# The first unit of the up projections with B22 third, x parts split from PSUM copies, weight sums ahead of the norm, and a later load of x in the down projections

## The chip, the core and the metric

The program runs on one core of one Trainium2 chip. The metric is the device time of one execution in microseconds (us), median of the runs shown. Six engines' rows appear below: PE (TensorE, matmuls), DVE (VectorE), ACT (ScalarE), POOL (GpSimd), SP (SyncE, which issues the DMAs); PEld is PE's weight load.

## What is computed

Two decoder layers over 1024 tokens with 1024 channels, all in float32. The feed-forward part of each layer, where the change lies, is, cut to what matters:

```python
def swiglu(h, w_gu, w_down):
    gu = h @ w_gu
    g, u = jnp.split(gu, 2, axis=-1)
    return (jax.nn.silu(g) * u) @ w_down

x = x + mixer(rms_norm(x, ...))          # layer 0: gMLP, layer 1: attention
x = x + swiglu(rms_norm(x, ffn_norm[l]), ffn_w_gu[l], ffn_w_down[l])
```

The width of g and of u is 2816 (22 blocks of 128 columns, 11 pairs).

## The kernel before

Every float32 operand is split in two: ACT makes `hi` (a rounded copy, `split` L162, L163), DVE makes `lo` = source - hi (L164), and PE does three matmuls for each product of blocks: hi hi, hi lo, lo hi. On top of that the projections use Strassen's scheme in Winograd's form: seven products instead of eight for a 2 x 2 split of the operands. On the side of x the seven operands are B11 and B21 (quarters of x), B22 (the fourth quarter), T1 = B11 - B12 and the sums T2, T3, T4 that are built on it; on the side of the weights a11, a12, a22 and S1 to S4, sums of quarters made on POOL (`sums` L324, `sum4` L336).

`ffn_up` (L242) goes over 11 pairs j of column blocks, for gate (gu = 0) and up (gu = 1). The first, j = 0, is the *first unit* (`unit` L353): it is computed product by product while the operands of x are still being made, since it follows the mixer's out projection and the norm. Later pairs (`pair` L450) find the operands ready. A product is 12 matmuls, 4 parts k by 3; a part needs hi and lo of that part (tiles such as T2h, T2l, by `put` L258) and the weights of the product (tile wg, hi and lo, by `weight` L300). The weights arrive in tiles `graw` (1 MB for each j and gu, two of them, `raw0` and `raw1`).

The norm is a scale of columns of x. `Entry` (L817) adds each finished tile of the out projection to x (`post`, L826), spills it (L827), squares it on ACT, and sums the squares on POOL, the last one on DVE (`Norm.add` L137). PE sums over partitions (`col`), DVE adds epsilon (nm, L146), POOL takes the power (nr, L150), PE spreads it as a row in PSUM, and `entry.scale` (L160, DVE) multiplies a tile of x by that row. There are two halves of tokens; B11 and B21 come from the first half, whose norm is ready early, the rest needs the second half's. The differences for T1 to T4 are taken in place on x by POOL (`difference` L263, L264; one, T2's last, on DVE).

What sets the order: a scheduler orders each engine's instructions by priority and dependence, and lists given to `T.order` fix DVE's and POOL's order around the first unit (L278 to L292, L549 to L565). Each engine runs its instructions in that order, so one that waits holds those behind it.

`ffn_down` (L604) multiplies the activations (in DRAM, `ascr`, written tile by tile by `store` L343 and `store_sums` L351) with the down weights, again in seven products. The first activation operand `a0` has two tiles, 5 blocks in `a0` and 6 in `a0b`; SP issues its loads, those of the weights and those of x (`new_x` L107, eight tiles of 512 KB from the spill `xscr`, L112) in one queue. The cuts hi and lo are L645 (ACT) and L646 (DVE), the sums of results into x are L681. Where x is loaded is one line:

```python
            with tc.issue_after(load(W4, weight(1, 1)).ins):
                xt = new_x(xscr)
            X = four(psp[0])
            product(X, A0, W2, True, 0, (W2, W3, W2))
            load(A0, act(2))
            add(X, 0, 0)
```

## Time and profile before

| | |
|---|---|
| median of 3 runs | 2198.87 us (2197.94 to 2204.6) |
| the profiled execution | 2199.69 us, its span 2198.0 |
| mean granted clock of PE | 0.988 |
| PE busy | 2111.9 us, 96% |
| DVE, ACT, POOL busy | 1444.8 (66%), 1213.7 (55%), 979.6 us (45%) |
| chain that ended last | PE 78%, DVE 12%, DMA 3% |
| matmuls | 10640 |
| DMA | 265.85 MB, mean 121 GB/s |

Times are from the start of the span. A row of a timeline has the start, the busy time, the engine and line, the operation, the tiles (out<-in) and, in brackets, the idle time of the engine before it with what released it. Busy times are shares over stages with different limits, so what a change is worth is read in its own stage. The granted clock is 1.00 at 2.4 GHz and 0.50 at 1.2 GHz.

### The profile page before, as it was taken

How to read it: one execution, taken by the hardware profiler on the slowest of the kernel's cores; microseconds unless marked ns; L12 is line 12 of the kernel's file. 1: busy time of each engine (PE TensorE's matmuls, PEld its weight loads, DVE VectorE, ACT ScalarE, POOL GpSimd, SP SyncE). 2: the span in 40 equal slices, each digit the busy share in tenths (PEclk: the TensorE clock that was granted, in tenths of full speed). 3: DMA queues.
4: the chain of work that ended last, by engine and by line, in shares of the span. 5: the costliest groups of instructions: out<-in, count | busy, mean ns of one | idle time of the engine just before them, and what ended most of it. 6: DMA issues, size and time to landing. Idle time of an engine off the chain costs nothing.

```text
span 2198.0 us, 30179 instructions
## 1 busy us (share of the span) xinstructions
PE 2111.9 (96%) x10640; PEld 1769.8 (81%) x10640; DVE 1444.8 (66%) x2541; ACT 1213.7 (55%) x2436; POOL 979.6 (45%) x856
## 2 busy tenths in 40 slices
PE   9999888999999979999999999999799999999998
PEld 7888666888888768878888888887588888887887
DVE  5545988545555656775288898865955555458685
ACT  5323355766676534453177777743466767664463
POOL 5023668675767400234122332204885757660024
PEclk9999999999999989999999999999999999999999
DMA  4230022232323853235423324573123223259413
GB/s 164 64 114 35 23 92 72 97 110 101 112 97 114 292 205 132 103 110 163 114 72 92 92 77 117 195 250 138 54 91 110 98 101 115 92 193 347 136 48 105
DMA packets 111320, 265.85 MB, mean 121 GB/s; under 512 B 10400, under 2 KB 20640, under 8 KB 104256
## 3 DMA queue, kind: packets, MB, share of 16 engines
q1 hardware_dynamic: 93808, 224.98, 29.5%
q0 software_dynamic: 17360, 38.93, 6.3%
q8 instruction: 84, 1.38, 0.3%
q14 instruction: 68, 0.56, 0.1%
HBM read 179.47 MB, written 77.07 MB: 117 GB/s over the span
## 4 chain that ended last, share of the span: by engine, by line
PE 78%; DVE 12%; DMA 3%; issue 2%; ACT 2%; POOL 2%; SPq 0%; DVEq 0%; POOLq 0%; ACTq 0%
PE mm L39 54%; PE d L39 15%; PE sc L39 3%; PE po L39 3%; PE tr L42 2%; DVE cut L646 1%; DVE wg L164 1%; DVE w_hi L164 1%; DVE w_lo L164 1%; DVE E L1241 1%; PE tr L39 1%; DMA x<-xscr 1%; DMA a0b<-ascr 1%; DVE fine L164 1%; DVE E L1253 1%
## 5 line engine op out<-in xcount | busy, mean ns | idle before, releaser
L39 PE MATMUL d<-cut 128*128 128x512 f32 (+1 forms) x1788 | 407.2, 388 | 24.2 <-ACT cut L645 15.0
L39 PEld LDWEIGHTS d<-cut 128*128 128x128 f32 x1788 | 331.8, 189 | 96.4 <-ACT cut L645 15.4
L137 POOL TENSOR_TENSOR acc<-acc,sq 128x512 f32<-128x512 f32 (+1 forms) x64 | 92.6, 1448 | 381.2 <-ACT sq L133 379.5
L462 DVE TENSOR_TENSOR c<-c,mm 128x256 f32<-128x256 f32 (+1 forms) x300 | 150.4, 507 | 159.0 <-PE mm L39 128.6
L309 DVE TENSOR_TENSOR wg<-row,wg 128x512 fp32r<-128x512 f32 x180 | 116.7, 658 | 91.8 <-ACT wg L308 87.9
L39 PE MATMUL mm<-hT_hi,w_hi 128*128 128x512 f32 x384 | 155.9, 406 | 0.0
L39 PE MATMUL mm<-hT_hi,w_lo 128*128 128x512 f32 x384 | 151.4, 394 | 0.0
L39 PE MATMUL mm<-hT_lo,w_hi 128*128 128x512 f32 x384 | 150.9, 393 | 0.0
L645 ACT CAST cut<-a 128x512 fp32r<-128x512 f32 x110 | 68.1, 621 | 138.5 <-PE d L39 136.2
L39 PE MATMUL mm<-fine,wg 128*128 128x256 f32 x960 | 138.0, 283 | 2.5 <-DVE c L462 1.2
L39 PEld LDWEIGHTS mm<-fine,wg 128*128 128x128 f32 x960 | 129.8, 190 | 12.9 <-ACT wg L308 2.6
L321 ACT COPY c<-mm 128x512 f32<-128x512 f32 x152 | 88.9, 585 | 80.3 <-PE mm L39 48.5
L646 DVE TENSOR_TENSOR cut<-a,cut 128x512 fp32r<-128x512 f32 x110 | 88.8, 807 | 61.1 <-ACT cut L645 60.8
L331 POOL TENSOR_TENSOR S<-graw 128x512 f32<-128x512 f32 x44 | 59.3, 1349 | 153.8 <-DMA graw<-in_w_gu 153.8
L39 PE MATMUL mm<-B11h,wg 128*128 128x512 f32 x352 | 118.7, 398 | 4.5 <-DVE wg L164 3.4
L39 PE MATMUL mm<-T1h,wg 128*128 128x512 f32 x352 | 117.4, 395 | 5.4 <-DVE wg L309 4.4
L308 ACT CAST wg<-S 128x512 fp32r<-128x512 f32 x160 | 98.4, 620 | 39.1 <-PE mm L39 31.0
L39 PE MATMUL mm<-B22h,wg 128*128 128x512 f32 x352 | 117.6, 396 | 2.2 <-DVE wg L164 1.8
L39 PE MATMUL mm<-T2h,wg 128*128 128x512 f32 x352 | 117.6, 396 | 0.5 <-DVE wg L164 0.5
L1245 ACT ACTIVATE E<-E,nm 128x256 f32<-128x256 f32 (+7 forms) x128 | 99.6, 778 | 33.3 <-DVE nm L1241 31.5
L308 ACT CAST wg<-graw 128x512 fp32r<-128x512 f32 x160 | 99.4, 623 | 32.0 <-PE mm L39 29.4
L350 POOL TENSOR_TENSOR c<-c,c 128x512 f32<-128x512 f32 x88 | 115.8, 1326 | 0.9 <-PE mm L39 0.7
(287 smaller groups left out, 5787.8 us busy)
## 6 DMA issues: line engine op xcount, KB each, us to landing
graw<-in_w_gu SPq DMA_DIRECT2D x44, 1024.0 KB, 4.9
ascr<-c SPq DMA_DIRECT2D x154, 256.0 KB, 2.0
a<-ascr SPq DMA_DIRECT2D x12, 1280.0 KB, 6.6
a<-ascr SPq DMA_DIRECT2D x18, 768.0 KB, 4.9
xscr<-x SPq DMA_DIRECT2D x48, 256.0 KB, 2.1
w<-in_w_down SPq DMA_DIRECT2D x14, 768.0 KB, 7.9
a0b<-ascr SPq DMA_DIRECT2D x12, 768.0 KB, 7.5
x<-xscr SPq DMA_DIRECT2D x16, 512.0 KB, 11.8
```

Source lines behind the costliest of these rows:

```text
L39: return self._keep(self.engine.matmul(*args, **kw))
L137: return (V if last else G).tensor_tensor(self.acc, self.acc, part, op=ALU.add)
L164: return V.tensor_tensor(lo, src, hi.bitcast(F32), op=ALU.subtract)
L308: A.copy(w[:, 0], src)
L309: T.note(line, name, V.tensor_tensor(w[:, 1], near, w[:, 0].bitcast(F32), op=ALU.subtract))
L321: A.copy(r, src)
L331: T.note(line, ("S1", layer, j, gu), G.tensor_tensor(s1, a21, a22, op=ALU.add))
L350: G.tensor_tensor(to, x, y, op=op_)
L462: V.tensor_tensor(c, c, ps, op=ALU.add)
L645: A.copy(o[:, 0], src)
L646: T.note(line, name + ("lo",), V.tensor_tensor(o[:, 1], src, o[:, 0].bitcast(F32), op=ALU.subtract))
L1245: A.activation(Em[:, :L], Em[:, :L], AF.Exp, scale=-1.0, bias=nm, accum_out=acc)
```

## The change

1. In the first unit the products come in the order B11, B21, B22, T1, T2, T3, T4 (before: B11, B21, T1, T2, T3, B22, T4). B22's part k is scaled by the norm and split at once; T2 then finds its tile scaled. The result c12 starts with B22's product, and T1's and T2's are added to it.
2. `put` gets a place `near` in PSUM for T1 to T4: ACT copies the part of x there as well, and DVE's split reads the copy instead of x in SBUF. The weights of T3 and T4 go the same way, as those of later pairs do.
3. All weight sums of j = 0 are made ahead of the norm in POOL's order; those of gu = 1 lie in a tile `early` that lends its room from T4 (layer 0) or T3 (layer 1), and the splits of B22's weights stand ahead of the scales on DVE.
4. `raw0` and `raw1` of layer 0 lie where room comes free early, and SP issues both `graw` loads ahead of all sixteen spills of x of the mixer (before: behind twelve). The splits of the weights of B11 and B21 then stand among the out projection's operands on DVE. In layer 1 they stand behind the third add on x instead of the second. The pool of weight tiles has 6 (layer 0) and 5 (layer 1) buffers instead of 4, and the accumulators of the squares have tiles of their own.
5. In both down projections x is loaded behind `load(A0, act(2))` instead of behind the load of W4.

The diff, without the parts that only follow from this (unchanged lists, the move of two definitions, and the old lists of order):

```diff
@@ -243,20 +243,29 @@
...
-            order = (("B11", "T1", "T2", "T3", "B22", "S", "w1", "s1"), ("s", "T4", "B21", "raw0", "raw1"))
+            order = (("B11", "T1", "raw0", "raw1", "T2", "T3", "B22", "w1"), ("T4", "s", "B21", "S", "s1"))
             if layer:
                 order = (("w1", "raw1", "raw0", "B11", "T1", "T2", "T3", "B21", "S"), ("T4", "s", "B22", "w2", "s1"))
-            ps = {n: (pool, right)[side](st, f"g{n}{layer}", {"w1": 4, "w2": 2}.get(n, 1)) for side in range(2) for n in order[side]}
+            ps = {n: (pool, right)[side](st, f"g{n}{layer}", {"w1": 5 if layer else 6, "w2": 2}.get(n, 1)) for side in range(2) for n in order[side]}
...
+            early_at = "T3" if layer else "T4"
...
-                hi[n] = p.tile([P, 4, 512], F32R, name=n + "h")
+                if n != early_at:
+                    hi[n] = p.tile([P, 4, 512], F32R, name=n + "h")
...
-            def put(n, k, src):
-                T.note(line, ("lo", layer, n, k), split(hi[n][:, k], lo[n][:, k], src))
+            early = ps[early_at].tile([P, 4, 4, P], F32, name="early", tag="early")
+
+            def put(n, k, src, near=None):
+
+                if near is not None:
+                    A.copy(near, src)
+                A.copy(hi[n][:, k], src)
+                src = src if near is None else near
+                T.note(line, ("lo", layer, n, k), V.tensor_tensor(lo[n][:, k], src, hi[n][:, k].bitcast(F32), op=ALU.subtract))
 
...
-                "B11": lambda k: entry.scale(k, 0), "B21": lambda k: entry.scale(k + 4, 0), "B22": lambda k: xt[k + 4][:, h1],
+                "B11": lambda k: entry.scale(k, 0), "B21": lambda k: entry.scale(k + 4, 0), "B22": lambda k: entry.scale(k + 4, 1),
...
-                "T2": lambda k: difference(("T2", k), xt[k][:, h0], entry.scale(k + 4, 1), xt[k][:, h0]),
+                "T2": lambda k: difference(("T2", k), xt[k][:, h0], xt[k + 4][:, h1], xt[k][:, h0]),
...
+            n_raw, n_stage = [0], [0]
+            spare = pool(st, "spare", 1, space=PSUM) if layer else None
+
+            def stage():
+                n_stage[0] += 1
+                return spare.tile([P, 512], F32, name="near") if layer and n_stage[0] % 2 else entry.row(0)
+
...
-                for n in ("B11", "B21", "T1", "T2"):
+                for n in ("B11", "B21", "B22", "T1", "T2"):
                     for k in range(4):
-                        put(n, k, sources[n](k))
+                        put(n, k, sources[n](k), stage() if n[0] == "T" else None)
...
                 w = (ps["w2"] if layer and name[-1] == "B22" else w1).tile([P, 2, *src.shape[1:]], F32R, name="wg")
-                if name[1] == layer and name[2] == 0:
+                if name[1] == layer and name[2] == 0 and name[-1] not in ("T3", "T4"):
...
@@ -327,7 +336,8 @@
...
-                s4, s3, s2, s1 = (sp.tile([P, 4, P], F32, name=n) for n in ("S4", "S3", "S2", "S1"))
+                s4, s3, s2, s1 = (sp.tile([P, 4, P], F32, name=n) if j or not gu else early[:, i]
+                                  for i, n in enumerate(("S4", "S3", "S2", "S1")))
...
+                sum4(0, gu, a12, s2, s4)
+                SRC[gu] = {"T3": s3, "T4": a22}
                 Z, Y, X = (p.tile([P, 512], F32, name="mm") for p in mmp)
                 product(X, a11, "B11", True)
                 c11 = snap(f"c11{gu}", X, 2 - gu)
...
+                product(Y, s4, "B22", True)
+                c12 = snap(f"c12{gu}", Y)
+                yield
                 product(Z, s1, "T1", True)
                 c22 = snap(f"c22{gu}", Z)
-                sum4(0, gu, a12, s2, s4)
+                T.note(line, ("c12", layer, 0, gu), V.tensor_tensor(c12, c12, Z, op=ALU.add))
                 yield
                 product(X, s2, "T2", False)
-                c12 = snap(f"c12{gu}", X)
+                V.tensor_tensor(c12, c12, X, op=ALU.add)
+                multiply(X, (yield), "T3", False, (layer, 0, gu, "T3"))
+                V.tensor_tensor(c22, c22, X, op=ALU.add)
+                multiply(X, (yield), "T4", False, (layer, 0, gu, "T4"))
+                res += [c11, c12, X, c22]
...
-                product(X, s3, "T3", False)
-                V.tensor_tensor(c22, c22, X, op=ALU.add)
-                yield
-                product(Z, s4, "B22", False)
-                V.tensor_tensor(c12, c12, Z, op=ALU.add)
-                yield
-                product(X, a22, "T4", False)
-                res += [c11, c12, X, c22]
...
+            SUMS, SRC = {}, {}
...
@@ -533,7 +544,7 @@
...
-            for b in ("B11", "B21", "T1", "T2"):
+            for b in ("B11", "B21", "B22", "T1", "T2"):
...
-            for n in ("T3", "B22", "T4"):
+            for n in ("T3", "T4"):
+                ws = [weight(SRC[gu][n], ("w", layer, 0, gu, n)) for gu in range(2)]
+                if n == early_at:
+                    hi[n] = ps[n].tile([P, 4, 512], F32R, name=n + "h", tag="early")
                 for k in range(4):
-                    put(n, k, sources[n](k))
+                    put(n, k, sources[n](k), stage())
                 for gu in range(2):
-                    next(first[gu], None)
...
+                    first[gu].send(ws[gu])
+            sc, lo_, w = (lambda k: ("scale", layer, 1, k)), (lambda n, k: ("lo", layer, n, k)), (lambda n, gu: ("w", layer, 0, gu, n))
...
+            names = [w("B22", 0), w("B22", 1), sc(4), sc(5), lo_("B22", 0), sc(6), sc(7), lo_("B22", 1), sc(0), c11_(0), lo_("B22", 2), sc(1),
+                     lo_("B22", 3), c11_(1), sc(2), sc(3), w("T1", 0), lo_("T1", 0), lo_("T1", 1), w("T1", 1), lo_("T1", 2), lo_("T1", 3), w("T2", 0)]
+            names += [lo_("T2", k) for k in range(3)] + [("d", layer, "T2", 3), lo_("T2", 3), w("T2", 1), c12_(0), c12_(1)]
+            for n in ("T3", "T4"):
+                names += [w(n, 0), w(n, 1)] + [lo_(n, k) for k in range(4)]
             T.order(line, names)
...
+            names = [("S4", layer, 0, 0)] + [(f"S{i}", layer, 0, 1) for i in (1, 2, 3, 4)]
+            names += [("d", layer, "T1", k) for k in range(4)] + [("d", layer, "T2", k) for k in range(3)]
+            names += [("d", layer, n, k) for n in ("T3", "T4") for k in range(4)]
...
             X = four(psp[0])
             product(X, A0, W2, True, 0, (W2, W3, W2))
-            load(A0, act(2))
+            with tc.issue_after(load(A0, act(2)).ins):
+                xt = new_x(xscr)
...
-        acc = hp[1].tile([P, 2, 512], F32, name="acc", tag="hT")
-        norms = [Norm(HALF[h], acc[:, h], sq) for h in range(2)]
+        norms = [Norm(HALF[h], tp.tile([P, 512], F32, name=f"acc{h}", tag=("vh", "vl")[h]), sq) for h in range(2)]
...
```

Three places in the order of instructions, before and after.

SP at the start of layer 0's down projection, before (w_6715 is W4, a_6711 the first tile of a0, a0b its second, a_6713 the tile of a1, c the stored results of the last pair of columns):

```order
L112 DMA x<-xscr_83 128x1024
L343 DMA ascr_87<-c_6311 128x512
L112 DMA x<-xscr_83 128x1024 x4
L343 DMA ascr_87<-c_6475 128x512
L112 DMA x<-xscr_83 128x1024
L351 DMA ascr_87<-c_6424 128x512
L112 DMA x<-xscr_83 128x1024 x2
L351 DMA ascr_87<-c_6369 128x512
L600 DMA a_6711<-ascr_87 128x5x512
L351 DMA ascr_87<-c_6495 128x512
L351 DMA ascr_87<-c_6497 128x512
L600 DMA a0b<-ascr_87 128x3x512 x2
```

and after:

```order
L361 DMA ascr_87<-c_6464 128x512
L353 DMA ascr_87<-c_6351 128x512
L361 DMA ascr_87<-c_6535 128x512
L361 DMA ascr_87<-c_6409 128x512
L611 DMA a_6751<-ascr_87 128x5x512
L353 DMA ascr_87<-c_6515 128x512
L361 DMA ascr_87<-c_6537 128x512
L611 DMA a0b<-ascr_87 128x3x512 x2
L611 DMA a_6753<-ascr_87 128x5x512
L611 DMA a_6753<-ascr_87 128x3x512 x2
L611 DMA a0b<-ascr_87 128x3x512
L112 DMA x<-xscr_83 128x1024 x8
```

The eight loads of x stood between the stores and ahead of the loads of a0b; they now stand behind all three loads of a0b, the last of which belongs to the third product.

DVE behind the norm of the second half in layer 0, before (row is the norm's row in PSUM, x_132 to x_135 the tiles of the fourth quarter, x_136 to x_139 those of the second):

```order
L146 TENSOR_SCALAR nm4_2336<-row_2331 128x4
L160 SCALAR_TENSOR_TENSOR x_136<-x_136,fgain0_333,row_2330 128x512
L160 SCALAR_TENSOR_TENSOR x_137<-x_137,fgain0_333,row_2330 128x512
L160 SCALAR_TENSOR_TENSOR x_138<-x_138,fgain0_333,row_2330 128x512
L160 SCALAR_TENSOR_TENSOR x_139<-x_139,fgain0_333,row_2330 128x512
L164 TENSOR_TENSOR wg_2563<-S1_2478,wg_2563 128x512
L164 TENSOR_TENSOR T1l_2408<-x_136,T1h_2407 128x512
L160 SCALAR_TENSOR_TENSOR x_132<-x_132,fgain0_333,row_2330 128x512
L164 TENSOR_TENSOR T1l_2408<-x_137,T1h_2407 128x512
L160 SCALAR_TENSOR_TENSOR x_133<-x_133,fgain0_333,row_2330 128x512
L164 TENSOR_TENSOR T1l_2408<-x_138,T1h_2407 128x512
```

and after:

```order
L146 TENSOR_SCALAR nm4_2337<-row_2332 128x4
L160 SCALAR_TENSOR_TENSOR x_132<-x_132,fgain0_333,row_2331 128x512
L160 SCALAR_TENSOR_TENSOR x_133<-x_133,fgain0_333,row_2331 128x512
L268 TENSOR_TENSOR B22l_2413<-x_132,B22h_2412 128x512
L160 SCALAR_TENSOR_TENSOR x_134<-x_134,fgain0_333,row_2331 128x512
L160 SCALAR_TENSOR_TENSOR x_135<-x_135,fgain0_333,row_2331 128x512
L268 TENSOR_TENSOR B22l_2413<-x_133,B22h_2412 128x512
L160 SCALAR_TENSOR_TENSOR x_136<-x_136,fgain0_333,row_2331 128x512
L375 TENSOR_TENSOR c110_2526<-c110_2526,mm_2509 128x512
L268 TENSOR_TENSOR B22l_2413<-x_134,B22h_2412 128x512
L160 SCALAR_TENSOR_TENSOR x_137<-x_137,fgain0_333,row_2331 128x512
L268 TENSOR_TENSOR B22l_2413<-x_135,B22h_2412 128x512
```

The splits of T1 from x were the first to follow; now B22's four parts do, with two scales ahead of each of the first two, and a sum of results among them.

POOL ahead of the same norm, before (acc the norm's accumulator, S the weight sums of gu = 0, nr4 the power):

```order
L137 TENSOR_TENSOR acc_1681<-acc_1681,sq_2317 128x512
L137 TENSOR_TENSOR acc_1681<-acc_1681,sq_2322 128x512
L331 TENSOR_TENSOR S1_2478<-graw_2473 128x512
L333 TENSOR_TENSOR S3_2476<-graw_2473 128x512
L150 TENSOR_TENSOR nr4_2338<-nm4_2336,mhalf_75 128x4
L332 TENSOR_TENSOR S2_2477<-S1_2478,graw_2473 128x512
L337 TENSOR_TENSOR S4_2475<-graw_2473,S2_2477 128x512
```

and after (early holds the sums of gu = 1):

```order
L341 TENSOR_TENSOR S1_2503<-graw_2498 128x512
L343 TENSOR_TENSOR S3_2501<-graw_2498 128x512
L342 TENSOR_TENSOR S2_2502<-S1_2503,graw_2498 128x512
L347 TENSOR_TENSOR S4_2500<-graw_2498,S2_2502 128x512
L341 TENSOR_TENSOR early_2417<-graw_2528 128x512
L137 TENSOR_TENSOR acc1_1682<-acc1_1682,sq_2313 128x512
L342 TENSOR_TENSOR early_2417<-early_2417,graw_2528 128x512
L343 TENSOR_TENSOR early_2417<-graw_2528 128x512
L137 TENSOR_TENSOR acc1_1682<-acc1_1682,sq_2318 128x512
L347 TENSOR_TENSOR early_2417<-graw_2528,early_2417 128x512
L137 TENSOR_TENSOR acc1_1682<-acc1_1682,sq_2323 128x512
L150 TENSOR_TENSOR nr4_2339<-nm4_2337,mhalf_75 128x4
```

Two sums stood between the last accumulation and the power; now eight stand among the last three accumulations.

## Rows read from the trace of the kernel before

**Rows 1.** PE's waits, whole run (engine, line, tile; releaser: us in all, times, longest)

```profile
PE d L39 <- ACT cut L645: 15.0, 1, 15.0
...
PE mm L39 <- DVE x L826: 3.8, 1, 3.8
```

**Rows 2.** Slices of the first unit, layer 0 (busy us, granted clock, DMA share, GB/s)

```profile
300.00:310.00 10.00, 5.98 (x17) 4.12 (x16) 10.00 (x14) 4.80 (x9) 6.05 (x5) 0.68 0.57 208
...
330.00:340.00 10.00, 6.65 (x16) 4.17 (x17) 10.00 (x10) 5.67 (x11) 8.17 (x6) 0.72 0.00 0
```

**Rows 3.** Timeline of PE, then of ACT, start of layer 0's down projection

```profile
754.90 13.01 PE L39 MATMUL d<-cut 128*128 128x512 f32 x56 [2.28 <-DVE cut L646]
782.88 7.38 PE L39 MATMUL d<-cut 128*128 128x512 f32 x20 [14.97 <-ACT cut L645]
...
782.21 1.66 ACT L645 CAST cut<-a0b 128x512 fp32r<-128x512 f32 x3 [13.65 <-DMA a0b<-ascr]
```

**Rows 4.** Timeline of SP's DMA issues, first unit and down projection, layer 0

```profile
295.85 0.81 SPq L328 DMA_DIRECT2D graw<-in_w_gu  x2
...
762.81 1.58 SPq L112 DMA_DIRECT2D x<-xscr  x2
...
769.81 1.53 SPq L600 DMA_DIRECT2D a0b<-ascr  x2
...
784.79 0.36 SPq L600 DMA_DIRECT2D a0b<-ascr  x1
```

**Rows 5.** Page, part 6: DMA issues (KB each, median us to landing)

```profile
a0b<-ascr SPq DMA_DIRECT2D x12, 768.0 KB, 7.5
x<-xscr SPq DMA_DIRECT2D x16, 512.0 KB, 11.8
```

**Rows 6.** Slice of the down projection's start, layer 0

```profile
750.00:790.00 40.00, 22.75 (x88) 17.92 (x87) 20.35 (x28) 9.40 (x17) 4.22 (x3) 0.79 1.04 397
```

**Rows 7.** Timeline of PE, first unit of layer 0

```profile
305.49 1.22 PE L39 MATMUL mm<-B11h,wg 128*128 128x512 f32 x2 [3.44 <-DVE wg L164]
...
319.94 0.40 PE L39 MATMUL mm<-T1h,wg 128*128 128x512 f32 x1
...
363.58 0.40 PE L39 MATMUL mm<-B11h,wg 128*128 128x512 f32 x1
```

**Rows 8.** Timeline of DVE, end of out projection and first unit, layer 0

```profile
295.11 0.68 DVE L164 TENSOR_TENSOR w_lo<-wo,w_lo 128x512 fp32r<-128x512 f32 x1
...
308.85 0.68 DVE L137 TENSOR_TENSOR acc<-acc,sq 128x512 f32<-128x512 f32 x1
...
314.57 2.72 DVE L160 SCALAR_TENSOR_TENSOR x<-x,fgain,row 128x512 f32<-128x512 f32 x4 [1.85 <-PE row L42]
...
331.76 1.75 DVE L164 TENSOR_TENSOR T2l<-x,T2h 128x512 fp32r<-128x512 f32 x1
```

**Rows 9.** Timeline of POOL, first unit of layer 0

```profile
313.80 1.27 POOL L332 TENSOR_TENSOR S<-S,graw 128x512 f32<-128x512 f32 x1
...
331.25 6.78 POOL L264 TENSOR_TENSOR x<-x 128x512 f32<-128x512 f32 x4
```

**Rows 10.** PE's waits, 301 to 370, layer 0

```profile
PE mm L39 <- DVE T2l L164: 3.7, 3, 2.4
PE mm L39 <- DVE T1l L164: 2.1, 3, 0.7
...
PE mm L39 <- DVE T4l L164: 1.5, 3, 1.1
```

**Rows 11.** Groups of ACT's instructions, copies into PSUM (busy us, mean ns, idle before)

```profile
L307 ACT COPY row<-S 128x512 f32<-128x512 f32 x80 | 47.2, 591 | 17.4 <-POOL S L332 9.5 <-DVE wg L309 5.5 <-POOL S L331 1.1
```

**Rows 12.** Timeline of DVE, out projection of layer 1

```profile
1494.27 6.20 DVE L164 TENSOR_TENSOR wg<-graw,wg 128x512 fp32r<-128x512 f32 x4 [7.13 <-ACT wg L163]
```

**Rows 13.** PE's waits, 1535 to 1600, layer 1

```profile
PE mm L39 <- DVE T2l L164: 3.4, 3, 1.9
...
PE mm L39 <- DVE T1l L164: 1.8, 3, 0.7
```

25 lines of the change are left out of this document (3 added, 22 removed).

## Prediction

> **What bounds the kernel now.** I read the page's shares first: PE is nearly always busy, so a change that leaves the matmuls as they are can only win back what PE waits, and what it loses at half clock. The table of PE's waits over the whole run comes next [rows 1]: one wait of 15.0 us for a cut on ACT stands alone, and one of 3.8 us for a sum of x. Both lie where this change works. The slices of the first unit of layer 0 [rows 2] show that PE there loses speed too: the granted clock is 0.68 in 300 to 310 and 0.72 in 330 to 340, while DVE is busy for 10.00 of 10 us in both. DVE sets the pace of this unit, and PE, which stutters behind it, drops to half clock.
>
> The 15-us wait is read from the start of layer 0's down projection [rows 3]: PE is through its last operands at 782.88 - 14.97 = 767.91; ACT's casts of the second part of `a0` (a0b) start at 782.21, after 13.65 us for a DMA. The issue times [rows 4] say why: the eight loads of x, the last two from 762.81, are issued ahead of the a0b loads at 769.81. They are 512 KB each [rows 5], 4.19 MB, and the DMA is full from 750 to 790, at 397 GB/s [rows 6], so all that is queued lands in its turn.
>
> **The change, part by part.** The sum is made against the profiled execution, 2199.69 us (span 2198.0 and 1.7 around it); the median shown, 2198.87, is 0.8 below.
>
> *Down projection, layer 0.* The x loads move behind a0b and the loads of the next product. The 4.19 MB at 0.397 MB/us are some 10.5 us that no longer stand ahead of a0b: it lands near 771.7 instead of 782.2, and PE's wait shrinks from 15.0 to some 4.5. **-10.5.** Upper bound of the gain: the whole wait, and the half clock behind it (20 matmuls take 7.38 us where 56 take 13.01 [rows 3], so 20 should take 4.65): -15.0 - 2.7 = -17.7. Lower bound: a0b's own issue doesn't come before 769.81, since the stores that it reads stay ahead of it, and it lands after a load's median of 7.5 us on the page [rows 5], at 777.3: -4.9. I take the value between, since the DMA was full for the whole stretch [rows 6]: bytes decide there, not issue times. x itself is needed at the first add on x, by the order behind the fifth operand of product 1. It is now issued behind the a0b load that stood at 784.79 [rows 4], some 10.5 earlier, about 774.3, and all eight land within 11.8 [rows 5], by 786. That add would come near 784 and needs the first of the eight: covered, but by a few us only; if the cover is gone, see the first rival. In layer 1 the same move meets no wait of size: 0, between -2 and +2.
>
> *Weights of the first two products, layer 0.* PE waited 3.44 for B11's weights, up to 305.49 [rows 7], and ran at half clock behind it (0.68 for that slice, so 3.2 of 10 us [rows 2], of which the wait itself has a part): some 6 in all. The loads of these weights stood at 295.85 on SP [rows 4], behind twelve spills of x; now they stand ahead of all of them, and the four splits on DVE stand among the operands of the out projection. If DVE has no gap in that stretch they cost 4 x 0.68 = 2.7 there (a split alone, the row at 295.11 [rows 8]); at 1.75, which a split takes beside POOL [rows 8], 7.0. I take 2.7, the nearer row, as it is of the same stretch.
>
> *The norm, layer 0.* Against this: POOL now makes eight weight sums among the norm's last three accumulations. The tiles of these sums come free with the split that ends at 295.8 [rows 8], or 298.5 with the 2.7 above. Eight sums and three accumulations of the same size, at 1.27 alone to 1.70 beside DVE (6.78 for four) [rows 9], are 14.0 to 18.7 us: POOL is through at 312.5 to 317.2, and the last accumulation on DVE, at 308.85 before [rows 8], comes 3.7 to 8.4 later. From there to the first scale at 314.57 [rows 8] lay 5.7 us, in part PE's other matmuls ahead of the norm's; I count 4.5 to 5. The first scale comes at 317 to 322, and the first product of B22 two later, at 319 to 324, where the third product began at 319.94 [rows 7]. PE has B11 and B21 (48 matmuls of 0.232 [rows 3], 11.1 us) until about 315, then it idles. Third product: -0.8 to +4.1, taken **+1.5**. What was won on B11's weights is thus spent before the norm.
>
> *From the third product to the next unit, layer 0.* Before: 319.94 to 363.58 [rows 7], 43.6 us for five products, 120 matmuls, of which 27.8 are due. The waits named T1l, T2l and T4l are 2.1, 3.7 and 1.5 [rows 10], 7.3 in all. A split of T2 from SBUF takes 1.75 beside POOL [rows 8]; scales, with a PSUM operand, take 0.68 each there (2.72 for four) [rows 8], although POOL starts its differences within them. So T1 to T4 with x read from PSUM come to about 0.65 each and these waits go, with half the lost clock of the slice 330 to 340 (0.28 of 10 us, so 1.4): about -9. Against it: B22, third now, keeps its splits from SBUF, and each part of it needs two scales and a split on DVE, 2 x 0.68 + 0.68 to 1.75 = 2.0 to 3.1 us, where PE takes 0.7: three waits of 1.3 to 2.4, +4 to +7. I take +4. **-5**, bounds -9 and +2. The sums for the T3 and T4 weights read PSUM as well; that's in the -9.
>
> *The copies.* Sixteen copies into PSUM per layer on ACT, and four for T3's and T4's weights, at 0.591 [rows 11]: 9.5 and 2.4 us of ACT, which is busy for 4.80 and 5.67 of 10 us [rows 2]. It hides them; without cover, the copy for the first part of each of T1 to T4 would show, 4 x 0.6 = 2.4 per layer. The two extra adds on c12 (0.6 each) end beside matmuls.
>
> *Layer 1.* DVE worked 6.20 us on four weight splits, which had waited 7.13 for ACT's casts of the loaded weights [rows 12], and the add on x for which PE waited 3.8 [rows 1] stood behind them. Now one more add stands ahead of the splits; the first part is there in time, so the 3.8 go, **-4** with a little clock (bounds -6 and 0). In the unit the waits for T2l and T1l are 3.4 and 1.8 [rows 13], -5.2, and some clock, -1.5; B22 costs +4 as above, and two more sums ahead of the norm (2 x 1.27 to 1.70) delay it by 2.5 to 3.4, of which 2.2 show: **-0.5**, bounds -7 and +6.
>
> Sum: -10.5 + 1.5 - 5 - 4 - 0.5 = -18.5: 2199.69 - 18.5 = 2181.2, less the 0.8 to the median: **2180.4 us**.
>
> **A rule weighed.** DVE's splits beside POOL take 1.75 and POOL's operations 1.70 instead of 1.27 [rows 8, 9]: both go on, one of each in turn, and a scale with a PSUM operand is not held (0.68). The Trainium skill ("SBUF — State Buffer", Who interferes with whom) has it harder: a DVE instruction with two SBUF inputs contends with a GpSimd one that reads SBUF, whoever issues first gets the shared pair for the whole instruction, and the other fully blocks. Taken as it stands, each of the eight sums ahead of the norm would hold one split of B21 or of the weights for its whole length, by an estimate 10 us a layer, and the sum would be near 2197, between the second and the third rival. The rows give the 1.5 and 2.2 counted above.
>
> **The rivals.**
> 1. *The down projection gains little.* a0b is not ahead of 769.81 (its lower bound, -4.9 instead of -10.5), or x now comes late and DVE, in order, holds product 1's cuts behind an add. x lands by 786 against a need near 784: up to 2, with 2.7 of half clock behind it. For it: 4.5 us of margin at most. Against: the first of eight lands long before the last. +5.6: **2186**. Chance 0.14.
> 2. *The first units gain nothing.* B22's splits and POOL's differences take turns at 1.75: B22 costs 7 instead of 4 in each layer, the norm's delay goes to its end in both (+2.6 and +1.2), and the half clock of one more pause is lost (2.7 [rows 3]): 6 + 3.8 + 2.7 = 12.5: **2193**. For it: POOL starts the T1 differences as soon as scales end. Against: it must first wait for the last four scales. Chance 0.12.
> 3. *Slower: POOL's sums hold the norm.* Eight sums and DVE's splits at 1.70, as [rows 8, 9] have wherever both run. Norm at its late end and beyond (+5.9 a layer), B22 at +3, and PE, idle for over 4 us ahead of B22, does B22's 24 matmuls at half clock, as after the 15-us wait (24 x 0.232 more [rows 3], 5.6): 14.5 a layer, 29 in two: **2209**. It decides from where PE idles for more than 4 us ahead of B22 in both layers. For it: B11 and B21 give PE only 11.1 us of cover. Against: half of DVE's operations there have a PSUM operand. Chance 0.08.
>
> **How the numbers follow.** Forecast 0.66, rivals 0.14, 0.12 and 0.08. About 0.3%, 6.6 us, is what a measurement of this kernel can tell from no change: faster means below 2192.3, which the forecast and the first rival give (0.80), within 0.3% the second (0.12), slower the third (0.08). The range: below, the upper bound of the down projection (-7.2), that of layer 1's add (-2) and half of what both units could still win (-2 and -3.2): 2166. Above, it takes in the first two rivals, with 3 us for the second's own costs, and leaves out the third: 2196.
>
> **What would show it.** Right: PE's longest wait at the start of the down projection is 3 to 6 us, and x is issued near 774; no wait for B11's weights, none over 2 for an add on x near 1500; T1l to T4l at 0.6 to 0.7 on DVE; PE idle before B22 by 3 to 6 us, and B22l now heads the waits. Wrong: a wait over 8 at the down projection, a new wait behind an add on x there, or a first unit in layer 0 that ends later than 363.58.

## The result, and the profile after

| | before | after |
|---|---|---|
| median of 3 runs | 2198.87 us | 2177.77 us (2176.03 to 2179.49) |
| ratio | | 0.989 [0.9871, 0.991] |
| profiled execution, its span | 2199.69, 2198.0 | 2177.77, 2176.0 |
| mean granted clock | 0.988 | 0.989 |
| PE, DVE, ACT, POOL busy | 2111.9, 1444.8, 1213.7, 979.6 | 2106.4, 1431.5, 1233.8, 971.2 |

The kernel became faster by 21.1 us, inside the range and 2.6 us below the forecast. The terms behind that number fared less evenly. A table of milestones on PE (the first or last matmul of a kind in its timeline, us) shows it best. The profile of a second execution of the changed kernel, taken with the experiments below, stands beside it (again), and the last two columns have the length of each stage less its length before:

| milestone on PE | before | after | again | stage, after | stage, again |
|---|---|---|---|---|---|
| first matmul of B11, layer 0 | 301.3 | 300.6 | 304.5 | -0.7 | +3.2 |
| last of the up projections, layer 0 | 744.0 | 741.7 | 745.5 | -1.6 | -1.7 |
| end of the down projection, layer 0 | 982.9 | 966.0 | 965.9 | -14.6 | -18.5 |
| first matmul of B11, layer 1 | 1532.0 | 1513.2 | 1512.0 | -1.9 | -3.0 |
| half-way through the up projections, layer 1 | 1767.9 | 1750.2 | 1748.6 | +1.1 | +0.7 |
| last of the down projection, layer 1 | 2191.1 | 2169.1 | 2173.8 | -4.3 | +2.0 |

Half-way is the start of the 1105th of their 2208 matmuls. The last of them is no milestone in layer 1: the changed kernel runs 28 matmuls of the down projection ahead of it and the kernel before 2, so 26 x 0.232, 6.0 us, would be booked to the wrong stage.

One program differs from itself by 4 to 6 us in three of the six stages, the first among them, so smaller differences there are not read as the change's. The two stages with the up projections repeat to 0.4 us in the changed kernel. The unit of layer 1 as it was before took 235.9, 233.6 and 236.0 us to that half-way mark in three kernels that share it (before, and x late alone and half of x early below), so a difference of 1 us there is not told from none.

**Down projection, layer 0.** The profile of the changed kernel, PE's timeline at the start (start, busy time, engine and line, tiles, and in brackets the idle time ahead and its releaser):

```profile
741.56 11.97 PE L39 MATMUL d<-cut 128*128 128x512 f32 x52
753.99 9.38 PE L39 MATMUL d<-cut 128*128 128x512 f32 x40 [0.46 <-DVE cut L657]
765.53 34.80 PE L39 MATMUL d<-cut 128*128 128x512 f32 x145 [2.16 <-ACT cut L656]
```

The 14.97 us of [rows 3] are 2.16 now, and the 2.28 ahead of them are 0.46. SP's issues in the same stretch:

```profile
732.30 1.47 SPq L611 DMA_DIRECT2D w<-in_w_down  x3
...
737.20 4.89 SPq L611 DMA_DIRECT2D w<-in_w_down  x3
...
754.50 4.78 SPq L611 DMA_DIRECT2D a0b<-ascr  x2
...
768.04 0.36 SPq L611 DMA_DIRECT2D a0b<-ascr  x1
768.44 8.28 SPq L112 DMA_DIRECT2D x<-xscr  x8
```

The two a0b loads are issued at 754.50, where [rows 4] have 769.81, and x at 768.44, 6 us ahead of the 774 that the prediction gave. The first add on x follows at 780.97 with no wait. The weight loads moved too, which the prediction had not counted: the timeline of before has all six in one row at 742.84, here three are at 732.30 and three from 737.20.

**First unit, layer 0.** PE's timeline of the changed kernel:

```profile
314.17 1.84 PE L39 MATMUL row<-mean,acc 128*128 128x1 f32 x8 [7.76 <-DVE acc L137]
...
325.22 0.44 PE L39 MATMUL mm<-B22h,wg 128*128 128x512 f32 x1
...
331.14 0.39 PE L39 MATMUL mm<-T1h,wg 128*128 128x512 f32 x1
...
343.01 0.50 PE L39 MATMUL mm<-T2h,wg 128*128 128x512 f32 x1 [1.94 <-ACT T2h L266]
...
356.39 0.47 PE L39 MATMUL mm<-T4h,wg 128*128 128x512 f32 x1 [1.99 <-DVE c L387]
```

PE stands still for 7.76 us, waiting for the last accumulation of the norm. B22 then begins at 325.22 and takes 5.92 us up to T1, which is its 24 matmuls and no wait. DVE, between its accumulation and B22's splits, and POOL, whose sums hold that accumulation up, together with the weight split that stands ahead of it on DVE:

```profile
312.33 1.09 DVE L164 TENSOR_TENSOR wg<-early,wg 128x512 fp32r<-128x512 f32 x1 [3.03 <-ACT wg L163]
313.34 0.68 DVE L137 TENSOR_TENSOR acc<-acc,sq 128x512 f32<-128x512 f32 x1
...
321.18 0.69 DVE L268 TENSOR_TENSOR B22l<-x,B22h 128x512 fp32r<-128x512 f32 x1
...
330.74 0.68 DVE L268 TENSOR_TENSOR T1l<-row,T1h 128x512 fp32r<-128x512 f32 x1
```

```profile
295.89 1.30 POOL L341 TENSOR_TENSOR S<-graw 128x512 f32<-128x512 f32 x1 [1.83 <-DVE w_lo L164]
297.15 1.75 POOL L343 TENSOR_TENSOR S<-graw 128x512 f32<-128x512 f32 x1
...
311.60 1.27 POOL L137 TENSOR_TENSOR acc<-acc,sq 128x512 f32<-128x512 f32 x1
...
324.53 1.30 POOL L273 TENSOR_TENSOR x<-x 128x512 f32<-128x512 f32 x1 [7.21 <-DVE x L160]
```

POOL works without a gap from 295.89 to 312.87 on eight sums and three accumulations. B22's split, both of its operands in SBUF, takes 0.69 at 321.18, since POOL waits for scales there (7.21). T1's split with its operand in PSUM takes 0.68, where T2's from SBUF took 1.75 in [rows 8].

The slices of that stretch (columns as in [rows 2]) show what the pause costs besides itself: the granted clock is 0.51 in the slice that begins at 310.

```profile
300.00:310.00 10.00, 5.14 (x22) 3.60 (x20) 9.30 (x11) 3.98 (x7) 9.92 (x7) 0.98 0.27 105
310.00:320.00 10.00, 5.83 (x20) 5.08 (x21) 3.40 (x6) 2.87 (x5) 3.90 (x4) 0.51 0.01 2
...
330.00:340.00 10.00, 8.53 (x36) 6.15 (x35) 9.78 (x12) 9.28 (x18) 10.00 (x8) 1.00 0.07 26
```

The slices from 300 and 330, at 0.68 and 0.72 before [rows 2], are at 0.98 and 1.00, and the half clock has moved to the norm and behind it: the slices from 340 and 350 are at 0.83 and 0.87, where they were at 0.94 and 1.00. Over 300 to 370 the granted clock is 0.88 now and was 0.90, so this unit won nothing on the clock as a whole.

**Layer 1.** PE waits there, of the changed kernel: for the accumulation, for the add that stands behind B22's weight splits on DVE, and for an add on x.

```profile
1485.88 0.50 PE L39 MATMUL tr<-ob,w_hi 128*128 128x512 f32 x1 [1.15 <-DVE x L837]
...
1520.76 1.32 PE L39 MATMUL tr<-mean,acc 128*128 128x1 f32 x8 [4.01 <-DVE acc L137]
...
1534.22 0.47 PE L39 MATMUL mm<-B22h,wg 128*128 128x512 f32 x1 [2.76 <-DVE c L375]
```

DVE's rows say why:

```profile
1513.99 5.05 DVE L268 TENSOR_TENSOR B21l<-x,B21h 128x512 fp32r<-128x512 f32 x3
1518.96 1.74 DVE L137 TENSOR_TENSOR acc<-acc,sq 128x512 f32<-128x512 f32 x1
...
1528.17 0.69 DVE L164 TENSOR_TENSOR wg<-early,wg 128x512 fp32r<-128x512 f32 x1 [5.30 <-ACT wg L163]
1528.78 1.40 DVE L160 SCALAR_TENSOR_TENSOR x<-x,fgain,po 128x512 f32<-128x512 f32 x2
```

Three splits of B21 stand ahead of the accumulation and take 1.68 each beside POOL's sums. Then DVE waits 5.30 us for the second weight tile of B22, whose sums POOL makes last, and the scales that are ready to go stand behind it.

### The profile page after: what moved, and what is told of

Its sections match the earlier page's. It is cut to its first block, busy times and chain, and to the rows that moved or that the text cites. A ratio compares the mean times of both kernels' runs of the same rounds, so it can differ in the third digit from the quotient of the medians.

```text
span 2176.0 us, 30210 instructions
## 1 busy us (share of the span) xinstructions
PE 2106.4 (97%) x10640; PEld 1772.0 (81%) x10640; DVE 1431.5 (66%) x2545; ACT 1233.8 (57%) x2476; POOL 971.2 (45%) x856
## 4 chain that ended last, share of the span: by engine, by line
PE 79%; DVE 11%; DMA 3%; ACT 3%; POOL 3%; issue 2%; SPq 0%; DVEq 0%; POOLq 0%; ACTq 0%
PE mm L39 55%; PE d L39 16%; PE sc L39 3%; PE po L39 2%; PE tr L42 2%; DVE E L1251 1%; DVE w_hi L164 1%; DVE cut L657 1%; DVE w_lo L164 1%; DVE E L1263 1%; DVE wg L164 1%; PE tr L39 1%; DMA raw<-in_w_z 1%; DVE x L160 0%; DVE cc L1262 0%
## 5 line engine op out<-in xcount | busy, mean ns | idle before, releaser
L473 DVE TENSOR_TENSOR c<-c,mm 128x512 f32<-128x512 f32 (+1 forms) x300 | 151.5, 508 | 200.1 <-PE mm L39 161.5
L318 DVE TENSOR_TENSOR wg<-row,wg 128x512 fp32r<-128x512 f32 (+1 forms) x184 | 119.0, 659 | 69.1 <-ACT wg L317 62.5
L39 PEld LDWEIGHTS mm<-fine,wg 128*128 128x128 f32 x960 | 131.8, 190 | 10.5 <-ACT c L330 0.9
L351 POOL TENSOR_TENSOR c<-c,c 128x512 f32<-128x512 f32 x80 | 105.3, 1316 | 35.5 <-ACT cut L656 24.3
L341 POOL TENSOR_TENSOR S<-graw 128x512 f32<-128x512 f32 x42 | 54.5, 1297 | 145.9 <-DMA graw<-in_w_gu 138.1
L39 PE MATMUL mm<-T3h,wg 128*128 128x512 f32 x352 | 116.3, 392 | 0.6 <-DVE c L385 0.5
```

The lines of the kernel that those rows point to most:

```text
L39: return self._keep(self.engine.matmul(*args, **kw))
L318: T.note(line, name, V.tensor_tensor(w[:, 1], near, w[:, 0].bitcast(F32), op=ALU.subtract))
L341: T.note(line, ("S1", layer, j, gu), G.tensor_tensor(s1, a21, a22, op=ALU.add))
L351: (G if j else V).tensor_tensor(g, g, u, op=ALU.mult)
L473: V.tensor_tensor(c, c, ps, op=ALU.add)
```

## The experiments

Ratios are against the kernel before on the same chip, where its median was 2206.33 for the first four runs, 2204.17 for the next four and 2202.2 for the last two.

### Which part gives the down projection's gain: x late alone, and all but x late

The kernel before with part 5 of the change alone:

```diff
-            with tc.issue_after(load(W4, weight(1, 1)).ins):
-                xt = new_x(xscr)
+            load(W4, weight(1, 1))
...
-            load(A0, act(2))
+            with tc.issue_after(load(A0, act(2)).ins):
+                xt = new_x(xscr)
```

> The kernel before with nothing but part 5, x loaded behind the first operand of the third product. Bytes theory (x's 4.19 MB stood ahead of a0b): PE's wait of 15.0 at layer 0's down projection falls to 2 to 5, the time falls by 12 to 17 with layer 1's part: about 2184. Order theory (what moved a0b by 17 us is also the earlier place of the loads of W3 and of the stores, which the rest of the change brought): the wait falls only to 4 to 7, the first wait of 2.28 stays, and the time is about 2188. If the first units carry the gain instead: about 2197.

The opposite, the changed kernel with x loaded where it was before (the same lines the other way round):

> The changed kernel without part 5: x is loaded behind W4 again. What is left of the gain is that of the first units: by the milestones of the two traces 0.7 + 1.6 in layer 0 and 1.9 + 1.1 in layer 1, so about 2193; PE's wait at layer 0's down projection is back at 13 to 15. Order theory: only half of the wait comes back (8 or less) and the time is about 2187.

Measured: x late alone 2196.38 us, ratio 0.9955 [0.994, 0.9971]; all but x late 2188.41, 0.9917 [0.9896, 0.9938]. That is 10.0 us less, where 12 to 17 were expected, and 17.9 less, where some 6 were. PE's timeline at the start of the down projection, first of the former, then of the latter:

```profile
756.23 13.00 PE L39 MATMUL d<-cut 128*128 128x512 f32 x56 [2.23 <-DVE cut L646]
773.95 26.30 PE L39 MATMUL d<-cut 128*128 128x512 f32 x105 [4.72 <-ACT cut L645]
```

```profile
758.52 9.40 PE L39 MATMUL d<-cut 128*128 128x512 f32 x40 [0.46 <-DVE cut L657]
779.27 20.89 PE L39 MATMUL d<-cut 128*128 128x512 f32 x85 [11.35 <-ACT cut L656]
```

The two waits added up, in the four kernels:

| | the rest as before | the rest as changed |
|---|---|---|
| x early | 17.25 | 11.81 |
| x late | 6.95 | 2.62 |

x late takes 10.3 us of waiting away without the rest and 9.2 with it: the forecast wait of 4.5 and the 10.5 us are there, at 4.72 and 10.3. (The 4.72 fits both of the ranges expected for x late alone; the 11.35 lies between those for its opposite.) The rest of the change takes another 4.3 to 5.4 away, for which the prediction had no term. The weight loads on SP say from where: with the rest they are issued at 736.84 and 741.74 where x is early, and in x late alone, as in the kernel before, in one row that begins at 744.21. B22's product no longer stands late in a unit, and the room that these weights take comes free with it; this reason is read from the rows and the order, and not tried by itself. The issue of a0b moved with both, in x late alone and then in all but x late:

```profile
763.54 0.93 SPq L600 DMA_DIRECT2D a0b<-ascr  x2
```

```profile
766.88 2.23 SPq L611 DMA_DIRECT2D a0b<-ascr  x2
```

Counted from the last matmul of the up projections it comes at 25.8 us in the kernel before, 18.1 with x late alone, 20.6 with all but x late and 12.8 in the changed kernel: x late brings it forward by 7.7 or 7.8, the rest by 5.2 or 5.3. From that issue to PE's restart all four take 10.4 to 13.1. So most of what x late wins, it wins by letting SP come to a0b earlier.

The waits are sharper than the times here. The two times add up to 27.9 us, more than the 24 of the whole change by its ratios (0.989 and, below, 0.9893): on top of the rest x late is worth 0.0024 to 0.0027, 5 to 6 us, where the intervals overlap. Where the rest wins 17.9 is not shown either: its profiled execution is 8.4 us below that of the kernel before, whose median on this chip is 6.6 above that profiled execution. The last down projection of x late alone is 5.2 us longer than that of the kernel before, with waits for the cuts near 2158. That is not put down to x: two executions of the changed kernel differ by as much there, for a reason that the last section shows.

### Bytes or issues: half of each tile of x early

The kernel before, with as many loads of x ahead of a0b as it has, eight, but each of half a tile:

```diff
             with tc.issue_after(load(W4, weight(1, 1)).ins):
-                xt = new_x(xscr)
+                xt = new_x()
+                for t in range(NT):
+                    nc.sync.dma_start(out=xt[t][:, HALF[0]], in_=xscr[t][:, HALF[0]])
...
-            load(A0, act(2))
+            with tc.issue_after(load(A0, act(2)).ins):
+                for t in range(NT):
+                    nc.sync.dma_start(out=xt[t][:, HALF[1]], in_=xscr[t][:, HALF[1]])
```

> The kernel before, with one half of each x tile (256 KB) loaded where x was loaded and the other half behind the first operand of the third product. Bytes theory: half of the bytes leave the front, so the wait of 15.0 falls by about 5, to 8 to 10, halfway to x_late_only. Issue theory (eight issues on SP, whatever their size, hold the loads of a0b): the wait stays above 13.

Measured: 2199.33 us, 0.9968 [0.9953, 0.9982]. PE's timeline:

```profile
754.60 13.00 PE L39 MATMUL d<-cut 128*128 128x512 f32 x56 [2.23 <-DVE cut L646]
777.85 22.46 PE L39 MATMUL d<-cut 128*128 128x512 f32 x91 [10.24 <-ACT cut L645]
```

With eight issues ahead the wait is 10.24, just above the 8 to 10 expected and about half way between 14.97 (all of x ahead) and 4.72 (none). The bytes that are queued ahead set it, not the number of issues. They act in good part through a0b's issue, at 765.90 here, which is 22.2 us behind the last of the up projections and so half way, too.

### What the PSUM copies are worth

The changed kernel without them, in both calls of `put`; the splits read x in SBUF:

```diff
-                        put(n, k, sources[n](k), stage() if n[0] == "T" else None)
+                        put(n, k, sources[n](k))
...
-                    put(n, k, sources[n](k), stage())
+                    put(n, k, sources[n](k))
```

> The changed kernel without the copies of x into PSUM: T1 to T4's splits on DVE read x in SBUF again (the weights of T3 and T4 keep theirs). If DVE beside POOL sets the pace of T1 to T4, each split takes 1.1 to 1.75 instead of 0.68 and the time rises by 4 to 8 (2182 to 2186). If the norm and ACT set it, by less than 2.

Measured: 2191.81 us, 0.9937 [0.9918, 0.9956]. That is 0.0044 to 0.0047 above the changed kernel's two ratios, about 10 us, more than expected; its interval is clear of the first of the two and overlaps the second. The splits on DVE, layer 0:

```profile
336.52 1.77 DVE L268 TENSOR_TENSOR T1l<-x,T1h 128x512 fp32r<-128x512 f32 x1
...
345.06 5.18 DVE L268 TENSOR_TENSOR T2l<-x,T2h 128x512 fp32r<-128x512 f32 x3
```

and the stretch of the unit, first without the copies, then the changed kernel:

```profile
300.00:380.00 80.00, 57.37 (x208) 43.46 (x208) 71.38 (x79) 37.54 (x68) 62.28 (x44) 0.85 0.13 50
```

```profile
300.00:380.00 80.00, 64.10 (x249) 49.08 (x248) 60.58 (x80) 52.03 (x96) 66.01 (x55) 0.89 0.17 63
```

Without the copies a split takes 0.9 to 1.77 us instead of 0.68, DVE is busy 10.8 us longer, and PE has 41 fewer matmuls in the same 80 us. With them ACT works 14.5 us more (52.03 against 37.54), and it has the room. (In this execution the unit begins 5.8 us later. Over 80 us from its first matmul DVE is busy 7.0 longer and ACT 12.5 less; the 41 matmuls stay.) The wait for T2h at 343.01 is no price of theirs: the kernel without copies has such waits too, 3.2 us for two, and they go with the last edit below, which moves a difference on DVE. From B11 to the last of the up projections the kernel without copies is 9.2 us longer than the changed one in layer 0 and 5.1 in layer 1.

### The norm's wait and the late weight split: each moved, and both

The changed kernel was run again on the same chip as the three that follow:

> The changed kernel itself, unaltered, beside the three below on one chip: the measure that they are held against. 0.989 of the time before.

It took 2180.84 us, 0.9893 [0.9856, 0.9929]. Then two edits of the order. One lets POOL accumulate for the norm ahead of most sums, and DVE accumulate ahead of the splits that it stood behind (in layer 0 of B22's weights, in layer 1 of B21):

```diff
+                names.insert(19, ("acc", 1, 1))
...
+            if not layer:
+                T.order(line, [("S1", 0, 0, 0), ("S3", 0, 0, 0), ("S2", 0, 0, 0), ("accp", 0, 1, 5), ("S4", 0, 0, 0),
+                               ("accp", 0, 1, 6), ("accp", 0, 1, 7), ("S1", 0, 0, 1)])
+                T.order(line, [("acc", 0, 1), ("w", 0, 0, 0, "B22")])
```

> The changed kernel with the norm's last accumulations ahead of most weight sums: in layer 0 POOL does two of the three accumulations before S1' and all of them before the other sums of gu = 1, and DVE does the last one ahead of the split of B22's weights; in layer 1 DVE does it ahead of the last two splits of B21. Theory (the eight sums on POOL hold the norm, and PE has nothing else): PE's wait of 7.8 for the accumulator in layer 0 falls to 2 or 3 and that of 4.0 in layer 1 to below 1; B22 starts 4 to 5 and 2 to 3 earlier; what reaches the end is 3 to 7. Rival (the sums of gu = 1 then come too late for B22's second product, or the splits behind take what is won): under 2.

The other puts the split of B22's second weights behind the scales:

```diff
-            names = [w("B22", 0), w("B22", 1), sc(4), sc(5), lo_("B22", 0), sc(6), sc(7), lo_("B22", 1), sc(0), c11_(0), lo_("B22", 2), sc(1),
+            names = [w("B22", 0), sc(4), sc(5), lo_("B22", 0), sc(6), sc(7), lo_("B22", 1), sc(0), c11_(0), lo_("B22", 2), w("B22", 1), sc(1),
```

> The changed kernel with the split of B22's weights for gu = 1 behind the third split of B22 on DVE instead of ahead of the scales. In layer 1 DVE's scales stood behind that split until 1528.8, although the norm's row was there by about 1524; theory: B22 there starts 3 to 4 earlier and PE's wait of 2.8 before it goes, 2 to 4 at the end. In layer 0 the split was over before the row came: nothing changes. Rival (B22's second product then waits for these weights): 0.

And both together:

> Both of the two edits above. If the norm was the late one in both layers and the weights only in layer 1, they add up: 5 to 10 below the changed kernel. If one covers the other in layer 1, 4 to 6.

Measured: the norm early 2176.73 us, 0.9874 [0.9852, 0.9896]; the weights late 2176.19, 0.9877 [0.9849, 0.9904]; both 2171.75, 0.9847 [0.9825, 0.987]. Against 2180.84 that is -4.1, -4.7 and -9.1. Each alone lies within the interval of the unedited kernel; both together do not, and all their runs (2168.1 to 2172.53) are below all of its runs (2175.64 to 2188.18). The two intervals still touch, so 9.1 is not sharp. PE's waits with the norm early, layer 0 and then layer 1:

```profile
311.74 1.39 PE L39 MATMUL row<-mean,acc 128*128 128x1 f32 x8 [3.05 <-DVE acc L137]
317.87 1.12 PE L42 MATMUL row<-ident,nr 128*128 128x128 f32 x4 [1.97 <-POOL nr L150]
...
1514.74 1.05 PE L39 MATMUL tr<-mean,acc 128*128 128x1 f32 x8 [0.68 <-DVE acc L137]
1520.66 1.11 PE L42 MATMUL po<-ident,nr 128*128 128x128 f32 x4 [3.36 <-POOL nr L150]
1531.49 0.47 PE L39 MATMUL mm<-B22h,wg 128*128 128x512 f32 x1 [2.50 <-DVE c L376]
```

The waits of 7.8 and 4.0 fall to 3.05 and 0.68, but 2.0 and 3.4 come back one step later, where the power (nr) now stands behind the sums on POOL: of 8.0 us less waiting, 5.3 turn into a new wait on the same queue. The edit moves the accumulation ahead of POOL's sums and of DVE's splits at once, so their shares are not told apart. With the weights late PE meets B22 of layer 1 like this:

```profile
1529.83 0.47 PE L39 MATMUL mm<-B22h,wg 128*128 128x512 f32 x1 [0.25 <-DVE c L375]
```

So the wait of 2.76 there was the weight split's, not B22's own operands'.

### Two more edits of the order: a start that moves and an end that doesn't

On top of both edits, the mean (nm) between B21's last two splits on DVE, the power one sum earlier on POOL, and the norm's matmuls later on PE:

```diff
-            for n, at in zip(("col", "row"), ((1, "B11", 0), (1, "B11", 2)) if layer else ((1, "B11", 1), (1, "B11", 3))):
+            for n, at in zip(("col", "row"), ((1, "B11", 0), (0, "B21", 1)) if layer else ((0, "B21", 1), (0, "B21", 3))):
...
-                T.order(line, [("acc", 0, 1), ("w", 0, 0, 0, "B22")])
+            T.order(line, [("acc", layer, 1), ("lo", layer, "B21", 2), (f"x{layer}", 1, "mean"), ("lo", layer, "B21", 3), ("w", layer, 0, 0, "B22")])
+            pow_ = [(f"x{layer}", 1, "pow")]
+            T.order(line, [("S4", 1, 0, 0)] + pow_ + [("S1", 1, 0, 1)] if layer else [("S3", 0, 0, 1)] + pow_ + [("S4", 0, 0, 1)])
```

> norm_weights, and the rest of the norm's chain unblocked: the mean (nm) stands on DVE between the last two splits of B21 instead of behind both, with the split of B22's first weights behind it; the power (nr) stands on POOL one sum earlier in each layer; on PE the column sums and the row come after parts of B21 that are ready, so that PE need not idle ahead of them. Theory (what is left before B22 is the norm's own chain, with PE idle for 3.0 + 2.2 in layer 0 and 0.7 + 3.4 in layer 1): these waits fall to under 2 in all, B22 starts 4 to 6 earlier in layer 0 and 2 to 3 in layer 1, and the time falls by 5 to 8 from norm_weights, to a ratio of about 0.982. Rival (DVE, not the norm, sets B22 and what follows, so the start moves and the end doesn't): under 2.

And T2's fourth difference, which DVE makes, ahead of T2's splits:

```diff
-            names += [lo_("T2", k) for k in range(3)] + [("d", layer, "T2", 3), lo_("T2", 3), w("T2", 1), c12_(0), c12_(1)]
+            names += [("d", layer, "T2", 3)] + [lo_("T2", k) for k in range(4)] + [w("T2", 1), c12_(0), c12_(1)]
```

> norm_mean, with T2's fourth difference on DVE ahead of T2's splits instead of behind the third. PE waited 1.9 and 1.5 for ACT's cast of that part. Theory: both waits go, 2 to 4 less. Rival (DVE is behind by as much in all: the splits are only shifted): under 1.

Measured: 2172.67 us, 0.9866 [0.9844, 0.9888], and 2170.21, 0.9855 [0.9835, 0.9875]; neither can be told from 0.9847, where 5 to 8 us less were expected of the first. B22 of layer 0 begins 21.0 us behind B11 instead of 22.6, but T4 begins 55.3 behind B11, where it was 53.8 without the move. In layer 1 half of the up projections is through 230.8 and 229.4 us behind B11, where it was 232.6. PE's timeline of the first of the two:

```profile
309.37 1.02 PE L39 MATMUL row<-mean,acc 128*128 128x1 f32 x8 [0.33 <-DVE acc L137]
...
321.50 0.47 PE L39 MATMUL mm<-B22h,wg 128*128 128x512 f32 x1 [3.30 <-DVE c L379]
```

The waits for the norm are all but gone, and PE waits 3.30 for the add on c11 instead, which stands behind B22's scales and splits on DVE and holds the PSUM tile that B22 wants. Ahead of T4 it waits 3.53 for ACT's cast of the weights. The second edit removes the waits for T2h and leaves 5.9 in both layers for that add and 5.1 for the one on c22. The bound has passed from the norm to DVE's adds and, in the first of the two, to ACT's casts. The version with both edits of the order above is the one to keep: 9.1 us below the changed kernel on one chip.

## Why the prediction was right, and where it was not

The forecast of -18.5 against -21.1 is closer than its terms are, and that closeness is luck. In the first profile layer 0's down projection gave 4.1 us more than its term and the end of layer 1 4.3 more, while the other three terms came 1.6 to 2.1 short each. The range was wide enough to hold such errors. By the stages of the table:

| term | forecast | measured (two executions) |
|---|---|---|
| down projection, layer 0 | -10.5 (-17.7 to -4.9) | -14.6, -18.5 |
| norm and third product, then on to the next unit, layer 0 | +1.5 - 5 = -3.5 | -1.6, -1.7 |
| out projection, layer 1 | -4 (-6 to 0) | -1.9, -3.0 |
| unit, layer 1 (to half-way) | -0.5 (-7 to +6) | +1.1, +0.7 |
| down projection, layer 1 (from half-way) | 0 (-2 to +2) | -4.3, +2.0 |

- **Down projection, layer 0.** The mechanism was right, bytes ahead of a0b in a full queue, and shown three times: by the edit alone (10.3 us of wait), by its opposite (9.2) and by half the bytes (10.24 of wait left). The term was too small because a0b's own place was taken as fixed. The lower bound said that its issue "doesn't come before 769.81"; it came at 754.50, as x's loads no longer held SP up ahead of it and the weight loads had moved up as well. So "bytes decide there, not issue times" is half right: the bytes decide, and for the most part by way of the issue time. The first rival, little gain here, is out.
- **The norm, layer 0.** "POOL is through at 312.5 to 317.2": it was at 312.87, the early end. The last accumulation on DVE was to come 3.7 to 8.4 later than 308.85, and came at 313.34, 4.5 later. Still the third product began at 325.22, outside the 319 to 324 of the text and 3.8 above the +1.5 of the term. The step that failed is "PE has B11 and B21 (48 matmuls of 0.232 [rows 3], 11.1 us) until about 315, then it idles": PE does not get to B21 at all, since the norm's column sums stand among B11's matmuls. It idles 7.76 us ahead of them and does the rest of B11 at the lower clock level, and B21's 24 matmuls come after that.
- **From the third product to the next unit, layer 0.** The term was -5, and from B22's start to the last of the up projections the kernel gained 2.3 + 5.3 = 7.6. Its part of -9 for the splits from PSUM holds in the main: T1l to T4l take 0.68 and PE's waits for T1l, T2l and T4l, 7.3 in all [rows 10], are 2.9 (1.5, 0.2 and 1.2); the 1.4 of clock that it counted was won in the slice from 330 and lost again behind it (0.83 and 0.87). The part of +4 for B22 failed: "three waits of 1.3 to 2.4" did not come: POOL stands still while the first two parts of B22 are split, and PE, late with B21, comes to B22 only 4 us after the first split began. What did come are waits of 1.94 for T2h and 1.99 for the add on c22, which no term had.
- **Layer 1.** The gain on the add on x was mis-sized: 1.15 of the 3.8 stays. The unit came 1.2 to 1.6 above its term, by errors that cancel: of the delayed norm, "of which 2.2 show" was too small, as the accumulation alone costs 4.01, and the split of B22's weights ahead of the scales, which the prediction did not follow to its source on POOL, another 2.76; the +4 for B22's own splits did not come. Taking the second wait away, and then both, brings the unit from 236.6 us to 233.4 and 232.6, where it was 235.9 before. The end of layer 1, 0 in the forecast, shows -4.3 and +2.0. Of the -4.3, 1.8 is a wait for a cut at the start of its down projection, which the kernel before and x late alone have and the changed kernel does not; the rest is not traced. The +2.0 has the 6 us more that the last section explains.
- **The second rival**, first units that gain nothing, has its title nearly met (-1.6 in layer 0, +0.7 to +1.1 in layer 1), but neither its price, 12.5 above the forecast, nor its reason: three of B22's four splits in each layer take 0.68 to 0.69, none 1.75.
- **The third rival** had its condition met (PE idle for over 4 us in both layers, 7.76 and 4.01) and its price was wrong: it had 24 matmuls at half clock in each layer and 3 us more for B22, where only the last matmuls of B11 in both layers and, in one of two executions, the first of B22 in layer 1 ran slow, and B22's splits cost PE no wait. It names a true loss all the same: the two edits of the order that undo it win 9.1 us.
- **The signs named.** Right: no wait for B11's weights, none over 2 for an add on x near 1500, splits of T1 to T4 at 0.68, no wait behind an add on x at the down projection. Wrong: "B22l now heads the waits" (it has none of size, the norm's accumulation does), the wait at the down projection is 2.2, below the 3 to 6, x is issued 6 us ahead of 774, and PE idles 7.76 in layer 0, not 3 to 6, and ahead of the norm's sums instead of B22. The sign for a miss, a first unit that ends after 363.58, was met: T4's last part comes at 366.0, and yet the up projections end 2.3 us earlier. It was no good sign, as 363.58 is the start of the next pair, whose products the changed order mixes with T4's.
- **The rule weighed.** Beside POOL, three splits of B21 took 5.05 us, one sum of POOL's and one split in turn, and without the copies T's splits took up to 1.77; with an operand in PSUM they took 0.68 beside the same POOL. The Trainium skill ("SBUF — State Buffer", Who interferes with whom) says that a DVE instruction with two SBUF inputs contends with a GpSimd instruction that reads SBUF, and that one with at most one SBUF input, outside DVE's 2-port modes, does not. On that the trace agrees. What the prediction worked out from it, 10 us lost in each layer ahead of the norm, did not come: in layer 0 the last accumulation came 4.5 later, and three of the eight sums took only 1.26 to 1.30. The rule spoke more for the copies than against the sums.

## What to carry to other kernels

Where a load is late in a full DMA queue, count the bytes that stand ahead of it, and move those that are needed later; then look at when the load itself is issued and what else stands in front, since the next thing in the queue sets the new time. An operand staged in PSUM by an idle ACT bought DVE more than it cost here, with POOL reading SBUF at the same time. Work that is made "ahead" for later must not stand, on any in-order engine, ahead of a short chain that everybody waits for: here a norm's sum, its power and its scales were each held once by sums or splits for weights that nobody needed yet.

## What the runs showed of the hardware that was not expected

- The lower clock level came behind a short wait in one execution and not in another of the same program. Behind the wait of 2.76 us for the add on c11 in layer 1, the changed kernel's B22 begins like this, and then, in the second execution, behind 2.50:

```profile
1534.77 0.82 PE L39 MATMUL mm<-B22h,wg 128*128 128x512 f32 x2
...
1535.81 1.05 PE L39 MATMUL mm<-B22h,wg 128*128 128x512 f32 x2
```

```profile
1533.99 0.47 PE L39 MATMUL mm<-B22h,wg 128*128 128x512 f32 x1 [2.50 <-DVE c L375]
...
1535.22 0.63 PE L39 MATMUL mm<-B22h,wg 128*128 128x512 f32 x2
```

  In the first, three matmuls took 1.04, 1.28 and 1.28 us there instead of 0.69, so some 1.5 us were lost besides the wait. From 1530 to 1540 the granted clock is 0.83 in the first and 1.00 in the second. The wait for the accumulation ahead of these rows is the same in both, 4.01 and 4.00; what decides between them is not shown.
- Which of DVE and POOL is held by the other can change between two executions of one program. In the last down projection DVE's cuts have both operands in SBUF, and POOL multiplies x in SBUF. The changed kernel's DVE and POOL, then those of the second execution:

```profile
2135.68 0.69 DVE L657 TENSOR_TENSOR kept<-w,kept 128x512 fp32r<-128x512 f32 x1
...
2139.93 4.80 POOL L817 TENSOR_TENSOR x<-x,near 128x512 f32<-128x512 f32 x1
```

```profile
2135.45 1.75 DVE L657 TENSOR_TENSOR kept<-w,kept 128x512 fp32r<-128x512 f32 x1
...
2134.94 1.72 POOL L817 TENSOR_TENSOR x<-x,near 128x512 f32<-128x512 f32 x1
```

  In the first POOL pays, in the second DVE, and PE then waits 4.1 us in all for its cuts, which it does not in the first; the stage is 6.2 us longer. The kernel before has it the first way; x late alone, x early and four of the five edits of the order have it the second way, and their last down projections are not to be held against its last one without that in mind.
- One program, run twice, reached its first unit at 300.6 and 304.5 us. Single profiles of this kernel can't carry a stage's difference of less than that.
